# A hybrid decoder layer on one core: three small inputs in one transfer, and another order of the instructions

## The chip, the cores and the metric

The kernel runs on 1 core of one Trainium2 chip. The metric is the device time of one execution in microseconds (us), the median of several runs; lower is better. The engines of the core are TensorE (PE; matrix products and transposes), VectorE (DVE), ScalarE (ACT), GpSimd (POOL) and SyncE (SP), which only issues transfers here.

## The reference

One layer over 1024 tokens of width 1024, in float32:

```python
mod = einsum('bd,de->be', silu(c), w_ada) + b_ada
shift, scale, gate = split(mod, 3)
h = rms_norm(x, norm_w) * (1.0 + scale) + shift
proj = einsum('bsd,de->bse', h, w_in)             # 2888 columns
u_pool, g_pool, q, k, v, g_attn, qi, ki, wi = split(proj, ...)
pool_out = pool_mixer(u_pool, w_pool, pool_scale) * silu(g_pool)
q = rope(rms_norm(q, q_norm_w)); k = rope(rms_norm(k, k_norm_w))
qi = rope(qi); ki = rope(ki)
# dsa_attention, per block of 128 queries (8 heads of 64 over 2 key/value heads):
score = einsum('bqhs,bqh->bqs', relu(qi . ki), wi)  # causal
sel = top_k(score, 256)                             # keys that a query may use
attn_out = softmax(q . k over sel) @ v * silu(g_attn)
y = concatenate([pool_out, attn_out]) @ w_out
x = x + gate * y
```

The pooling mixer takes causal means over windows of 2, 4, 8 and 16 tokens, less the token itself, and one 128 x 128 map for each of 4 groups.

## The kernel before, in words

Tokens are worked on in 8 tiles of 128, or in halves of 512 columns (tiles 4 to 7 first, then 0 to 3). Products that must stay exact are split: a value is cast to its high part (`wh`, `hhi`, `qsh`, `mph`, `xh`) and the rest is the low part (`wl`, `hlo`, `qsl`, `mpl`, `xl`), and each product is three: hi by hi, hi by lo, lo by hi.

Nothing of the order on the engines is written out. Each part of the work is a generator ("strand") that hands its next instruction to a planner, the class `Flow`. The planner keeps a clock for each engine and a cost for each instruction, and issues the one that can start first, corrected by numbers: `EARLY` (by strand, or by strand and its count), `LAST` and `SAFE` (for PE), `FAVOUR` (where an instruction may go to DVE, ACT or POOL, `Either`), `COLD` (until when PE counts as slow), `HOP`, `PHOP`, `STT`, `SWITCH` (small costs), `XB`, `FK`, `MIX`, `AHEAD` (how far loads, products and buffers may run ahead). So a change of one number can move instructions anywhere, and which engine takes one of an `Either`. All instructions are issued from one line of a helper, L238 in the profile of before.

The work goes in this order:

- **Head.** The x tiles 7 to 4 (`xr`) are loaded, squared and summed (`sq`), scaled by their RMS and transposed on PE (`m<-c,xr`). The adaLN sums run on DVE, one pass over each `wada` tile (`wa`), two tiles for each of 8 blocks j; `lead_loads` (L612) issues these pairs, and puts the loads of the x tiles 3 to 0 ahead of pair j = `XB`. `query_loads` brings the weights of the lead line (`ld<-wq`). With shift and scale, h becomes `hhi` and `hlo`, and the lead line multiplies them by the index-query weights: 512 columns for the first half, 256 for part of the second. `c`, `norm_w` and `b_ada` are loaded as `cT`, `nwT` and `badaT`.
- **Keys, values and index queries.** `wkh`, `wkl` by `hhi`, `hlo` give keys, values, index keys (`st`, then `twice` and `kiT`) and index weights. The index queries (`qix`, 4 tiles of 768 columns) are rotated: a shuffle `sw<-qix`, a product with cos, one with sin and the sum, then split into `xh`, `xl`.
- **Gates, queries, mixers.** `ORDER` sets their sequence. Meanwhile, index scores are summed, and the 256 best keys found by bisection: passes that count keys over a limit (`junk` on DVE for tiles 2, 3 and 4: 384, 512 and 640 columns; `ajunk` on ACT for tiles 5, 6 and 7), with small steps (`aq`, `yq`, `xq`) between. For each query group e, the squares are summed on PE: `m<-qsh,c` and `m<-qsl,c`, from a half's `qsh` cast and `qsl` difference. The sums of q2, q1 and q0 follow each other, q0's first. The mixers use `u`, `nx`, `gp` and end in `mph`, `mpl`.
- **Attention** of units 0 to 7: products `m<-kT,qr`, maxima and masking on DVE (`ex`, `mx`), exponentials on ACT (`ex`), transposes (`m<-c,ex`), copies of them (`pw`), products with v, gates (`gt`, `st`, `mah`, `mal`).
- **Output.** `m<-mph,wh` and the like for the pooled half, `m<-mah,wh` for the attended, added into `xo` on DVE.

Of the kernel before, what the change touches and what calls it, by code (L numbers as in the profile page):

```python
# [27 lines left out]
ORDER = "a0 a2 a1 q2 q1 | q0 m1 q3 m2 m3 m0 a3"  # L28
SWAP16 = [(i + 16) % 32 for i in range(32)]
GROUPS = (((5, 6, 7), True), ((2, 3, 4), False))  # L30
# [32 lines left out]
         "lead_out 1": -0.38, "shift 8": 1.56, "out 7": -0.3, "unit 3": -1.17, "turns 3": -3.11,
         "key_value_out 1": -2.25, "exps 4": -0.27, "mix 2": -0.2, "exps 2": 0.46, "out 6": -0.73, "gated 8": -2.42,
         "out 5": -2.76, "token_turns": -1.26, "token_out 9": -0.19, "h_half 14": -0.44, "h_half 10": -0.92,
# [1557 lines left out]
```

## Time and profile before

| what | value |
|---|---|
| time, median of 3 runs | 511.67 us (511.54 to 512.37) |
| profiled execution, its own time | 511.55 us |
| its span in the trace | 509.7 us |
| granted clock of PE, mean | 0.99 |
| busy: PE, DVE, ACT, POOL | 482.0, 417.9, 381.8, 152.0 us |
| moved by transfers | 58.36 MB, mean 114 GB/s |

The span is what the profiler sees of one execution; the time holds 1.85 us more around it. Busy times are averages over very different stretches. The granted clock says at which of two levels PE ran: 1.00 is 2.4 GHz and 0.50 is 1.2 GHz.

### The profile page before, as it was taken

The page shows a single profiled execution, that of the slowest core. Times are in us where ns is not written, and L with a number is a line of the kernel's source. Part 1 is how long each engine was busy: PE and PEld are TensorE (multiplying, and loading weights), DVE is VectorE, ACT ScalarE, POOL GpSimd, SP SyncE. Part 2 cuts the span into 40 slices and gives each one's busy share as a digit, 9 for nine tenths or more (in the row PEclk, how much of TensorE's full clock was granted, in tenths as well). Part 3 has the DMA queues.
Part 4 walks back from the last instruction along what each step waited for, and adds up shares of the span by engine and source line. Part 5 has one row for each costly group of instructions (what it writes and reads, how often), then busy time and mean ns, then how long its engine had stood idle before and what let it go on. Part 6 is the DMA issues. An engine that isn't in the chain of part 4 may idle for free.

```text
span 509.7 us, 8516 instructions
## 1 busy us (share of the span) xinstructions
PE 482.0 (95%) x2912; PEld 361.2 (71%) x2912; DVE 417.9 (82%) x910; ACT 381.8 (75%) x879; POOL 152.0 (30%) x182
## 2 busy tenths in 40 slices
PE   1899999999999989999999998999998999998996
PEld 1678999776768857877887775886675648654485
DVE  5977897799789789989999999978989896666342
ACT  3896541697778999999935999899997666669410
POOL 3597062002001133476131236613521232400000
PEclk9899999999999999999999999999998999999999
DMA  8998503010205112111120013675632134421054
GB/s 300 410 408 311 185 14 119 22 54 31 76 8 186 42 42 84 41 42 42 42 65 27 34 42 92 198 270 163 186 107 64 34 112 124 166 63 43 1 168 163
DMA packets 27884, 58.36 MB, mean 114 GB/s; under 512 B 3776, under 2 KB 7872, under 8 KB 27840
## 3 DMA queue, kind: packets, MB, share of 16 engines
q1 hardware_dynamic: 27840, 57.81, 33.3%
q8 instruction: 23, 0.38, 0.3%
q14 instruction: 21, 0.17, 0.1%
HBM read 47.32 MB, written 10.49 MB: 113 GB/s over the span
## 4 chain that ended last, share of the span: by engine, by line
PE 82%; DVE 8%; DMA 5%; ACT 3%; issue 1%; POOL 0%; SPq 0%; DVEq 0%
PE m L238 82%; DMA wa<-wada 4%; DVE ex L238 3%; ACT ex L238 2%; DVE junk L238 1%; DMA xr<-xR 1%; DVE selw L238 1%; DVE mpl L238 0%; DVE wa L238 0%; DVE mx L238 0%; DVE xq L238 0%; DVE xo L238 0%; DVE gp L238 0%; DVE st L238 0%; POOL qsl L238 0%
## 5 line engine op out<-in xcount | busy, mean ns | idle before, releaser
L238 PE MATMUL m<-hhi,wh 128*128 128x512 f32 (+1 forms) x320 | 120.0, 397 | 1.7 <-ACT xt L238 1.0
L238 PE MATMUL m<-hlo,wh 128*128 128x512 f32 (+1 forms) x320 | 115.2, 383 | 0.0
L238 PE MATMUL m<-hhi,wl 128*128 128x512 f32 (+1 forms) x320 | 115.0, 383 | 0.0
L238 ACT ACTIVATE ajunk<-key,xq 128x768 bf16<-128x768 uint16 (+2 forms) x93 | 96.4, 1036 | 1.5 <-DVE xq L238 0.3
L238 PEld LDWEIGHTS m<-hhi,wh 128*128 128x128 f32 x320 | 58.8, 188 | 18.5 <-issue 4.3
L238 POOL TENSOR_TENSOR wl<-ld,wh 128x512 fp32r<-128x512 f32 x42 | 60.5, 1443 | 38.2 <-ACT wh L238 18.8
L238 DVE TENSOR_SCALAR_CACHE_REDUCE junk<-key,xq 128x384 bf16<-128x384 uint16 (+2 forms) x93 | 69.2, 744 | 2.3 <-DVE xq L238 0.2
L238 PEld LDWEIGHTS m<-hhi,wl 128*128 128x128 f32 x320 | 59.2, 190 | 12.4 <-issue 1.7
L238 PEld LDWEIGHTS m<-hlo,wh 128*128 128x128 f32 x320 | 58.9, 190 | 11.8
L238 ACT ACTIVATE ex<-ex,mx,c 128x384 f32<-128x384 f32 (+7 forms) x64 | 54.9, 860 | 6.4 <-DVE mx L238 4.3
L238 DVE SCALAR_TENSOR_TENSOR score<-kt,c,score 128x1024 f32<-128x1024 f32 (+5 forms) x42 | 40.7, 970 | 7.1 <-ACT kt L238 4.9
L238 ACT ACTIVATE kt<-m 128x512 f32<-128x512 f32 (+1 forms) x80 | 37.7, 525 | 10.9 <-DVE score L238 5.0
L238 PE MATMUL m<-kT,qr 64*128 64x512 f32 (+3 forms) x192 | 40.0, 516 | 1.0 <-DVE mx L238 1.0
L238 DVE SCALAR_TENSOR_TENSOR xo<-m,c,xo 128x512 f32<-128x512 f32 x24 | 18.0, 750 | 25.4 <-PE m L238 18.4
L238 ACT CAST wh<-ld 128x512 fp32r<-128x512 f32 x31 | 19.2, 624 | 23.8 <-DMA ld<-wout 7.5
L238 DVE CUSTOM_DVE_ANT_0 ex<-m,key 128x512 f32<-128x512 f32 (+1 forms) x48 | 30.8, 662 | 5.0 <-PE m L238 4.8
L238 PE MATMUL m<-pw,vrow 128*64 128x512 f32 x144 | 33.3, 604 | 0.0
L238 POOL TENSOR_SCALAR wh<-ld 128x512 fp32r<-128x512 f32 x26 | 17.5, 672 | 51.7 <-PE m L238 33.4
L238 PEld LDWEIGHTS m<-kT,qr 64*128 64x128 f32 x192 | 20.4, 190 | 16.1 <-issue 10.6
L238 ACT COPY pw<-m 128x512 f32<-128x512 f32 x51 | 26.5, 595 | 5.7 <-PE m L238 5.5
L238 PEld LDWEIGHTS m<-c,ex 64*128 64x128 f32 x576 | 21.0, 138 | 10.9 <-DVE mx L238 3.7
L238 PE MATMUL m<-c,ex 64*128 64x64 f32 x576 | 24.0, 226 | 3.8 <-DVE mx L238 1.8
(198 smaller groups left out, 1025.6 us busy)
## 6 DMA issues: line engine op xcount, KB each, us to landing
wa<-wada SPq DMA_DIRECT2D x24, 512.0 KB, 9.3
ld<-wet SPq DMA_DIRECT2D x16, 512.0 KB, 3.4
ld<-wout SPq DMA_DIRECT2D x24, 256.0 KB, 3.2
xr<-xR SPq DMA_DIRECT2D x8, 512.0 KB, 7.3
xo<-xT SPq DMA_DIRECT2D x16, 256.0 KB, 3.8
y_d<-xo SPq DMA_DIRECT2D x16, 256.0 KB, 2.4
xo<-y_d SPq DMA_DIRECT2D x16, 256.0 KB, 3.2
outT<-xo SPq DMA_DIRECT2D x16, 256.0 KB, 2.4
```

The lines of the kernel that those rows point to most:

```text
L238: self.fn(*self.args, **self.kw)
```

## The change

Three small inputs become one array of 128 rows and 40 columns (c in columns 0 to 7, norm_w in 8 to 15, b_ada in 16 to 39), loaded by one transfer in the place of the first. The arithmetic stays, and PE has the same number of matmuls. The rest of the diff changes numbers of the planner. `ATT` (with `turn_of` and `firsts`) writes down the order of the attention units and of the two output halves, which is the one of before.

```diff
-ORDER = "a0 a2 a1 q2 q1 | q0 m1 q3 m2 m3 m0 a3"
+ORDER = "a0 a2 a1 q1 q2 | q0 m1 q3 m2 m3 m0 a3"
+ATT = "0 1 2 3 4 5 6 7"
...
-         "mix": -0.33, "rotated": 0.23, "query_loads": 0.21, "exps": -0.11, "score_sums": -1.07,
+         "mix": -0.33, "rotated": 0.62, "query_loads": 0.2, "exps": -0.11, "score_sums": -1.07,
...
-COLD = 17.877
+COLD = 18.869
-XB = 2
+XB = 3
...
-FK = 0
+FK = 1
-MIX = 5
+MIX = 4
-AHEAD = 4
+AHEAD = 5
-FAVOUR = {"DVE": 0.245, "ACT": -0.111, "POOL": 0.27}
+FAVOUR = {"DVE": 0.267, "ACT": -0.111, "POOL": 0.27}
...
-    c_sb = const([P, 8], F32)
+    c_all = const([P, 40], F32)
+    c_sb, nw_sb, bada_sb = c_all[:, 0:8], c_all[:, 8:16], c_all[:, 16:40]
-    nw_sb = const([P, 8], F32)
-    bada_sb = const([P, 24], F32)
...
-                yield SP.dma_start(c_sb, cT)
-        yield SP.dma_start(nw_sb, nwT)
-        yield SP.dma_start(bada_sb, badaT)
+                yield SP.dma_start(c_all, cT)
```

Of the changed numbers, some 70 stand in `EARLY`, `SAFE` and `LAST`. What they do shows in the order on the engines. Rows of before name line L238, rows of the change L241; the numbers behind names are those of buffers, and differ between the two.

**SP's queue in the head.** From `nwT` (c_77) to the last of the x tiles 3 to 0, before:

```order
L238 DMA c_78<-badaT 128x24
L238 DMA wa_147<-wada 128x1024
L238 DMA wa_149<-wada 128x1024
L238 DMA ld_151<-wq 128x1024
L238 DMA wa_152<-wada 128x1024
L238 DMA wa_159<-wada 128x1024
L238 DMA xr_161<-xR 128x1024
L238 DMA xr_166<-xR 128x1024
L238 DMA xr_173<-xR 128x1024
L238 DMA xr_176<-xR 128x1024
L238 DMA wa_274<-wada 128x1024
```

and in the change, from the first wada pair on:

```order
L241 DMA xr_112<-xR 128x1024
L241 DMA wa_143<-wada 128x1024
L241 DMA wa_145<-wada 128x1024
L241 DMA ld_147<-wq 128x1024
L241 DMA wa_148<-wada 128x1024
L241 DMA wa_153<-wada 128x1024
L241 DMA wa_258<-wada 128x1024
L241 DMA wa_260<-wada 128x1024
L241 DMA ld_262<-wq 128x1024
L241 DMA xr_263<-xR 128x1024
L241 DMA xr_269<-xR 128x1024
```

The two small transfers are gone, and the third wada pair (wa_258, wa_260) and the wq tile ld_262 stand ahead of the x tiles (xr_263 on) now, not behind them. On PE, 32 lead products of 512 columns stand between the first transposes and the second, where 20 did.

**POOL at the index queries**, behind the last work of the lead line, before:

```order
L238 TENSOR_TENSOR wl_619<-ld_474,wh_618 128x512
L238 TENSOR_TENSOR sw_751<-sw_751,sin_538 128x768
L238 TENSOR_TENSOR qix_726<-qix_726,sw_751 128x768
L238 TENSOR_TENSOR wl_856<-ld_712,wh_855 128x512
L238 TENSOR_TENSOR wl_898<-ld_742,wh_897 128x512
L238 TENSOR_TENSOR wl_921<-ld_742,wh_920 128x512
```

and in the change:

```order
L241 TENSOR_TENSOR hlo_650<-xt_440,hhi_649 128x512
L241 TENSOR_TENSOR qix_732<-qix_732,cos_500 128x768
L241 TENSOR_TENSOR sw_741<-sw_741,sin_502 128x768
L241 TENSOR_TENSOR qix_749<-qix_749,cos_500 128x768
L241 TENSOR_TENSOR sw_766<-sw_766,sin_502 128x768
L241 TENSOR_TENSOR qix_732<-qix_732,sw_741 128x768
L241 TENSOR_TENSOR qix_749<-qix_749,sw_766 128x768
L241 TENSOR_TENSOR qix_722<-qix_722,cos_500 128x768
L241 TENSOR_TENSOR sw_746<-sw_746,sin_502 128x768
L241 TENSOR_TENSOR wl_934<-ld_719,wh_933 128x512
```

POOL had two products of the rotations, of one index query (qix_726), and now has eight, of three index queries. DVE keeps the shuffles, the sum for qix_722 and the fourth index query.

**DVE at the norms of q0**, from the cast of its first half to the cast of its second half and what follows, before:

```order
L238 CAST qsh_1964<-st_2025 128x512
L238 TENSOR_TENSOR qsl_1965<-st_2025,qsh_1964 128x512
L238 TENSOR_SCALAR junk_2028,cq_315_2017<-key_83,xq_312_2010 128x512
L238 TENSOR_SCALAR junk_2044,cq_315_2017<-key_84,xq_312_2010 128x640
L238 TENSOR_TENSOR aq_324_2055<-cq_315_2017,kcq_250_1779 128x3
L238 SCALAR_TENSOR_TENSOR xq_325_2056<-aq_324_2055,yq_326_2057 128x3
L238 TENSOR_SCALAR junk_2077,cq_330_2076<-key_82,xq_325_2056 128x384
L238 TENSOR_SCALAR junk_2079,cq_330_2076<-key_83,xq_325_2056 128x512
L238 CAST qsh_1964<-st_2091 128x512
L238 TENSOR_SCALAR junk_2084,cq_330_2076<-key_84,xq_325_2056 128x640
L238 TENSOR_SCALAR yq_341_2102<-xq_325_2056 128x3
```

and in the change:

```order
L241 CAST qsh_1959<-st_2030 128x512
L241 TENSOR_TENSOR qsl_1960<-st_2030,qsh_1959 128x512
L241 TENSOR_TENSOR aq_317_2020<-cq_311_2003,kcq_248_1775 128x3
L241 SCALAR_TENSOR_TENSOR xq_318_2021<-aq_317_2020,yq_319_2022 128x3
L241 TENSOR_SCALAR junk_2050,cq_323_2049<-key_80,xq_318_2021 128x384
L241 TENSOR_SCALAR junk_2060,cq_323_2049<-key_81,xq_318_2021 128x512
L241 TENSOR_SCALAR junk_2063,cq_323_2049<-key_82,xq_318_2021 128x640
L241 TENSOR_TENSOR aq_332_2079<-cq_323_2049,kcq_248_1775 128x3
L241 CAST qsh_1959<-st_2093 128x512
L241 TENSOR_TENSOR qsl_1960<-st_2093,qsh_1959 128x512
L241 SCALAR_TENSOR_TENSOR xq_333_2080<-aq_332_2079,yq_334_2081 128x3
```

Before, the second cast (qsh_1964<-st_2091) stood between two scans (junk) of a pass, and its difference qsl was POOL's. Now the cast (qsh_1959<-st_2093) stands behind a whole pass, and the difference follows it on DVE. Between this cast and the second `mpl` (the one for which PE waits at 318 us), DVE issues one scan of 640 columns, three `yq`, one `nx` of 1016 columns, one `wl` and one `aq` less than before, and three `qsl` and one `wh` more.

Near the end, DVE's `gt` of unit 5, which stood just ahead of the last maxima of unit 6's heads, now stands behind four of them, and two copies of `pw` of the last unit go from DVE to ACT.

## Rows read from the trace of the kernel before

**Rows 1.** The page: busy time of each engine; the chain that ended last.
```profile
PE 482.0 (95%) x2912; PEld 361.2 (71%) x2912; DVE 417.9 (82%) x910; ACT 381.8 (75%) x879; POOL 152.0 (30%) x182
...
PE 82%; DVE 8%; DMA 5%; ACT 3%; issue 1%; POOL 0%; SPq 0%; DVEq 0%
```

**Rows 2.** Windows: stretch, length, busy us of each engine (instructions), granted clock, DMA share, GB/s.
```profile
24.00:60.00 36.00, 34.60 (x246) 29.38 (x245) 27.90 (x52) 26.67 (x44) 22.53 (x20) 1.00 0.84 307
...
30.00:100.00 70.00, 69.68 (x456) 63.71 (x456) 57.37 (x86) 39.06 (x89) 28.15 (x20) 1.00 0.47 166
...
190.00:305.00 115.00, 114.98 (x492) 90.34 (x490) 110.46 (x244) 99.46 (x249) 43.55 (x57) 0.99 0.14 46
305.00:320.00 15.00, 12.67 (x66) 9.15 (x65) 14.61 (x48) 14.87 (x38) 9.32 (x7) 1.00 0.39 110
```

**Rows 3.** Timeline of PE, head: start us, duration, engine, instruction, idle before.
```profile
25.27 0.72 PE L238 MATMUL m<-c,xr 64*128 64x64 f32 x16 [0.49 <-POOL xr L238]
...
59.11 0.32 PE L238 MATMUL m<-wkh,hhi 128*128 128x328 f32 x1
```

**Rows 4.** Timeline of PE at the first query norms.
```profile
188.24 0.39 PE L238 MATMUL m<-qsh,c 128*8 128x512 f32 x1 [0.75 <-DVE qsh L238]
189.59 0.45 PE L238 MATMUL m<-qsl,c 128*8 128x512 f32 x1 [0.95 <-POOL qsl L238]
189.84 0.63 PE L238 MATMUL m<-qsh,c 128*8 128x512 f32 x1
...
193.24 0.39 PE L238 MATMUL m<-hhi,wh 128*128 128x512 f32 x1
```

**Rows 5.** Waits of PE, 305 to 320 us: total us, times, longest.
```profile
PE m L238 <- DVE mpl L238: 1.4, 1, 1.4
PE m L238 <- DVE mx L238: 1.0, 2, 0.5
```

**Rows 6.** Waits of PE, 436 to 490 us.
```profile
PE m L238 <- ACT ex L238: 1.3, 2, 0.8
```

**Rows 7.** Timeline of SP's queue (SPq), its DMA issues in the head.
```profile
3.12 0.44 SPq L238 DMA_DIRECT2D c<-nwT  x1
3.60 0.43 SPq L238 DMA_DIRECT2D c<-badaT  x1
...
16.07 4.17 SPq L238 DMA_DIRECT2D wa<-wada  x4
```

**Rows 8.** Timeline of DVE, 12.67 us.
```profile
12.67 1.21 DVE L238 SCALAR_TENSOR_TENSOR wa<-wa,m 128x1024 f32<-128x1024 f32 x1
```

**Rows 9.** Timeline of POOL, DVE, ACT and PE around the index queries.
```profile
63.60 2.62 POOL L238 TENSOR_TENSOR sw<-sw,sin 128x768 f32<-128x768 f32 x1 [13.57 <-DVE sw L238]
...
88.53 1.63 DVE L238 TENSOR_TENSOR st<-st,rows 128x128 f32<-128x128 f32 x5 [2.75 <-ACT st L238]
...
90.97 1.06 ACT L238 COPY twice<-st 128x1024 f32<-128x1024 f32 x1 [2.39 <-DVE st L238]
...
93.25 0.92 PE L238 MATMUL m<-c,twice 128*128 128x128 f32 x7
```

**Rows 10.** Timeline of DVE and POOL at the query norms.
```profile
182.71 0.69 DVE L238 TENSOR_TENSOR qsl<-st,qsh 128x512 fp32r<-128x512 f32 x1
...
187.76 0.42 DVE L238 CAST qsh<-st 128x512 fp32r<-128x512 f32 x1
...
188.26 1.27 POOL L238 TENSOR_TENSOR qsl<-st,qsh 128x512 fp32r<-128x512 f32 x1 [1.88 <-DVE qsh L238]
```

**Rows 11.** Groups of DVE by form, 186 to 316 us: busy us, mean ns, idle before.
```profile
L238 DVE TENSOR_SCALAR_CACHE_REDUCE junk<-key,xq 128x640 bf16<-128x640 uint16 x24 | 21.1, 878 | 0.5
...
L238 DVE TENSOR_SCALAR yq<-xq 128x3 f32<-128x3 f32 x3 | 1.9, 631 | 0.0
...
L238 DVE TENSOR_TENSOR nx<-nx 128x1016 f32<-128x1016 f32 x1 | 1.2, 1212 | 0.0
```

**Rows 12.** Timeline of DVE, 438.60 us.
```profile
438.60 0.68 DVE L238 TENSOR_TENSOR gt<-gt,m 128x512 f32<-128x512 f32 x1
```

More of the change, by code (lines that the diff above doesn't have):

```diff
@@ L44 @@
+         "key_value_out": -1.34, "index_queries": -0.86, "norm": -0.31, "gate_loads": -1.2, "token_scales": -3.22,
+         "gate_mods": -0.39, "unit": -1.06, "index_scores": -1.07, "lead_loads": 1.31, "out": -1.44,
+         "lead_out": -0.62, "weight_loads": 0.29, "key_value_weights": -1.29, "main_line": 0.11, "output_line": 1.37,
          "turns": -1.46, "finish": -1.64, "index_keys": -1.47, "h_block": 0.28, "attention_keys": -0.36,
-         "turned": -1.0, "h_blocks": -0.59, "gated": -2.15, "modulations": 0.89, "low": 0.65, "gear": 0.42,
@@ L63 @@
[L63 to L65 removed]
[6 rows of a table added]
+         "key_value_out 6": -2.24, "norm 1": -1.96, "gear 4": -1.05, "products": -1.29, "shift 4": -0.32,
+         "norm 5": -1.64, "low 1": -2.52, "turns 6": -2.43, "gated 6": -2.43, "turns 8": -1.76, "h_block 3": -0.55,
@@ L75 @@
+         "token_out 13": -0.78, "token_out 5": -0.25, "h_half 7": -0.24, "token_tile 7": -0.74, "token_tile": -0.49,
+         "unit 5": 0.1, "unit 1": -0.94, "h_half 5": -0.42}
 SELECT = -0.425
-LAST = {"main": 0.12, "fill": -0.081, "scores": 0.035, "attend": -0.104, "evac": -0.027, "qi": 0.257,
-        "side": -0.376}
-SAFE = {"side": 1.0, "unit": 0, "query_norms": 0.69, "h_block": 0.59, "rotated": 0.48, "query_loads": 0,
-        "norm": 0.29, "weight_loads": 0.85, "key_value_out": 0.39, "turned": 0.26, "finish": 0, "index_keys": 0.85,
+LAST = {"main": 0.12, "fill": -0.081, "scores": 0.035, "attend": -0.104, "evac": -0.106, "qi": 0.257,
+        "side": -0.237}
@@ L81 @@
+SAFE = {"side": 1.0, "unit": 0, "query_norms": 0, "h_block": 0.59, "rotated": 0.48, "query_loads": 0,
+        "norm": 0.29, "weight_loads": 1.12, "key_value_out": 0.39, "turned": 0.26, "finish": 0, "index_keys": 1.01,
         "main_line": 0, "output_line": 0, "gate_mods": 1.06, "selection": 0, "low": 0.27, "maxima": 0,
-        "attention": 0.44, "lead_out": 0, "score_relus": 0, "lead_loads": 0.28, "score_sums": 0.18, "mix": 0.96,
-        "main": 0, "modulations": 0.09, "out": 0.39, "turns": 0.34, "exps": 0, "lead_line": 1.22, "shift": 0,
@@ L91 @@
+        "weight_splits": 0, "token_turns": 0, "gear": 0, "key_value_weights": 0}
+COLD = 18.869
+XB = 3
 WKM = 8
 HOP = 0.103
-PHOP = -0.1
-STT = 0.071
+PHOP = -0.148
+STT = 0.073
 HOPS = {"PE": 0.19, "DVE": 0.13, ("ACT", "DVE"): 0.14, ("ACT", "ACT"): 0.035}
-SWITCH = {"all": 0.1, "rows": 0.28, "columns": 0.29}
+SWITCH = {"all": 0.1, "rows": 0.28, "columns": 0.27}
 AGE = 0.37
@@ L1278, in hybrid_layer @@
     mixa, gate, done, normed, ended = {}, {}, [], [], []
+    turn_of = [int(i) for i in ATT.split()]
+    firsts = [c for c in (0, 1) if turn_of[-1] // 4 != c]
     main_over = []
@@ L1285, in gate_loads @@
         yield lambda: len(gates_out) == 8
-        for i in range(NT):
-            yield lambda: len(ended) >= i - 1
+        for n, i in enumerate(turn_of):
+            yield lambda: len(ended) >= n - 1
             t = yield big(w=512, s="gt", keep=keep)
@@ L1293, in attention @@
         yield lambda: kT and len(queries_out) == 4 and normed_q
-        for i in range(NT):
-            yield lambda: i in masks and len(ended) >= i - FLY
+        for n, i in enumerate(turn_of):
+            yield lambda: i in masks and len(ended) >= n - FLY
             flow.spawn(unit(i), "attend")
@@ L1365, in turns @@
         def turns():
-            yield lambda: len(done) >= i
+            yield lambda: len(done) >= turn_of.index(i)
             flow.spawn(products(), "attend")
@@ L1460, in project_attended @@
         cs = slice(c * 512, (c + 1) * 512)
-        yield lambda: len(ended) >= 4 * c + 4 and len(pooled_out) == 16
+        yield lambda: all(i in ended for i in range(4 * c, 4 * c + 4)) and len(pooled_out) == 16
         hi, lo = ([mixa[c][g][t][:, e * 512:(e + 1) * 512] for g in range(2) for e in range(2)] for t in range(2))
@@ L1492, in output_line @@
         yield from project_pooled()
-        yield from project_attended(0)
-        yield from project_attended(1)
+        yield from project_attended(firsts[0])
+        yield from project_attended(1 - firsts[0])
     flow.now(constants())
```

33 lines of the change are left out of this document (15 added, 18 removed), and 20 rows, old and new, of the table EARLY.

## The prediction

> **What bounds the kernel now.** I first read the page's busy times and its chain: TensorE (PE) is busy 482.0 of 509.7 us and holds 82% of the chain that ended last; VectorE (DVE) holds 8% and transfers 5% [rows 1]. So the time is PE's work, which the change leaves alone (its count of matmuls stays), plus the places where PE waits or runs at half clock. Then I cut the span into stretches to find those places. From 30 to 100 us PE is busy 69.68 of 70.00 us, from 190 to 305 it is busy 114.98 of 115.00; there, DVE is nearly as full, 110.46 us [rows 2]. What is left over lies in four places, and in each I went to the timeline and the chain of waits:
>
> 1. The head. The second half of the tokens (tiles 3 to 0) is turned on PE from 25.27 us, and the first key/value product (wkh) starts at 59.11 [rows 3]. Between 24 and 60 us PE idles only 36.00 - 34.60 = 1.40 us [rows 2].
> 2. The first query norms. PE waits 0.75 us for DVE's cast qsh and 0.95 us for qsl, which POOL computes; then, from 189.84 to 193.24, eight norm products take 0.425 us each at half clock [rows 4].
> 3. The first attention units and the pooled output, 305 to 320 us. PE waits 1.4 us for mpl and 1.0 us for two maxima, all of them DVE's [rows 5].
> 4. The end of the attention, where PE waits twice for exponentials, 1.3 us together [rows 6].
>
> The profiled execution took 511.55 us, 0.12 below the median of 511.67, so the sum is made on 511.55. A change of under 0.2%, or 1.02 us, can't be told from none.
>
> **The change part by part.**
>
> *The merged transfer.* Two issues on SP go, 0.44 and 0.43 us, 0.87 together [rows 7]. That all of it arrives at the end I don't expect: DVE takes the first wada tile at 12.67 without a wait ahead of it, straight behind its own scaling of x [rows 8], and the tiles follow at the pace of their bytes. Between 0 and 0.87 us, I take 0.4, the middle, for the arrival of later tiles.
>
> *The moved x tiles.* The four loads of x tiles 3 to 0 go behind the third wada pair and one wq tile: on SP's queue three loads of 512 KB each pass them. SP issues four such loads in 4.17 us once the queue is full [rows 7], so one takes (4.17 - 0.43) / 3 = 1.25 us and three 3.74. The second transposes then start 3.74 us later, less the 0.4, at about 28.6. PE isn't idle for all of that, because twelve more of the lead products stand ahead of the transposes in its order now (32 instead of 20). They are 512 columns wide like the norm products, which take 0.425 us at half clock [rows 4], so 0.2125 at full: 2.55 us. From the transposes on the work is as before, less those twelve: 59.11 moves by 3.74 - 0.4 - 2.55 = **+0.8 us**. Bounds: -0.6, if in the new order PE loses none of its 1.40 us of idle time in that stretch; +2.5, if the clock falls once more while PE has work (rival 2). From 30 us on PE has no spare time [rows 2], so this passes on to the end.
>
> *The index-query rotations.* Three sine products, three cosine products and two sums go to POOL or stay there; POOL had two such before, of 2.62 us the first, after 13.57 us with nothing to do [rows 9]. PE is busy with other products to 93 us, so this costs nothing as long as POOL's chain ends in time. What that needs is rival 3.
>
> *The norms of q0.* POOL needed 1.27 us for the second qsl, after DVE's cast of 187.76; DVE needs 0.69 us for the same shape [rows 10]. Now DVE does cast and qsl one after the other, so that the last of them ends near 187.76 + 0.42 + 0.69 = 188.9 instead of 189.5, and PE goes on 0.7 us earlier. Of PE's two waits the second shrinks from 0.95 to about 0.3, and its idle time here from 1.70 to 1.05. In the stretch from 305 to 320 us it idles 1.4 in one piece and 1.0 in two [rows 5], and the granted clock stays at 1.00 [rows 2]. So I expect no fall here, which saves half of 193.24 - 189.84, or 1.7 us: together -2.4. If the clock falls all the same, -0.7.
>
> *What DVE loses after it.* A gain of PE at place 2 holds only if DVE comes earlier at place 3 too, because all PE's waits there are for DVE. DVE hardly idles between [rows 2], so its own sum decides. From the cast of q0's second half to mpl, counted in the order of both kernels, it issues one scan of 640 columns (junk), three yq, one nx of 1016 columns and one wl less: 0.88 + 3 x 0.63 + 1.21 + 0.69 = 4.67 us, the wl at the price of the qsl of the same shape; and three qsl and one wh cast more: 3 x 0.69 + 0.42 = 2.49 us, the wh at the price of the cast qsh [rows 10, 11]. Net -2.2. PE's -2.4 and DVE's -2.2 are nearly the same size, so the waits of place 3 stay as they are, and what reaches the end is the smaller: **-2.2 us**. It is also about this if the clock does fall at place 2, since the waits of place 3 (2.4 us) then shrink by what DVE gains and PE doesn't. Bounds: -2.4, and -0.7 if DVE's gain is eaten up, by waits for ScalarE at the norms of q3 or by POOL's port.
>
> *The tail.* DVE's gt of 0.68 us stood ahead of the maxima of unit 6 at 438.60 [rows 12], and now stands behind four of them; two copies of pw at the end go to ScalarE. Bounds: 0, if ScalarE's exponentials start when PE lets them, and -1.3, both waits of [rows 6]. I take **-0.4**, below the middle, since PE sets the start of most of what ScalarE does there.
>
> Sum: 511.55 + 0.8 - 2.2 - 0.4 = 509.75, so **509.8 us**.
>
> By the Trainium skill ("DMA: Bandwidth & Descriptors", Rules for kernel authors) many small transfers should become one large one, and those under 64 KB are mostly overhead: by it the whole 0.87 would come through, and the sum would be 509.3; the trace shows only that much of issue time on SP, not that it is waited for.
>
> **The rivals.**
>
> *1. Place 2 gives little.* The clock still falls there, and DVE's removed work is filled by waits for ScalarE. Then 511.55 + 0.8 - 0.7 - 0.4 = 511.25, within 0.2%. For it: 0.75 us of the waits at place 2 come from DVE's cast, which now stands behind one more scan. Against it: DVE's own sum.
>
> *2. A second fall in the head.* With x later, PE idles before the second transposes, and if the clock falls when PE has work again, half a stretch like the 3.4 us at place 2 [rows 4] is lost: +1.7, so 511.45, within 0.2%. It needs work without a break from the fall on; before the transposes, PE would wait for x anyway and the loss be hidden.
>
> *3. POOL's rotations come late: slower.* Eight products of 768 columns now stand on POOL before DVE can finish the third index query (qix_722 in the order). At 1.5 times the 1.27 us of 512 columns [rows 10] they take 8 x 1.9 = 15.2 us and end at 63.6 + 15.2 = 78.8. DVE then has nine instructions ahead of its st, of 0.69 us (512 columns) to 1.5 times that (768), some 8.5 us: 87.3, ahead of 88.53, when it started st after waiting 2.75 us for ScalarE. At the 2.62 us that the row of POOL shows, they end at 84.6 and st starts at 93.1, 4.6 late. ScalarE's copy twice, made from st, ended at 92.03, and PE took it at 93.25 [rows 9]: a cushion of 1.2. So PE loses 3.4 us there and all behind it is later: 509.75 + 3.4 = 513.15, slower by 0.3%. It decides from 8.5 + 63.6 + 8 t = 88.53 + 1.2 on, a product of t = 2.2 us. For it: the one row of POOL at this width. Against it: that row lies beside DVE's own products, of which few are left while DVE waits for POOL. The Trainium skill ("GPSIMD Engine Reference", Engine selection) advises against two-input elementwise work on POOL, as about twice as slow as on DVE; the trace agrees at 512 columns, 1.27 against 0.69 us [rows 10]. Twice 1.5 times 0.69 would be 2.1, and the chain just in time.
>
> *4. The merge does all it can.* The whole 0.87 us reaches the second transposes, the rest as in the sum: 509.75 - 0.47 = 509.3.
>
> **How the numbers follow.** The sum as it stands 0.42, rival 4 0.15: faster 0.57. Rivals 1 and 2, 0.13 and 0.09: same 0.22. Rival 3 and the upper bounds of the other terms together 0.21: slower. The lower end is the sum with each term near its better bound, 511.55 - 0.6 - 2.4 - 1.3 = 507.25, so 507.3; the upper end is rival 3, 513.2. The likeliest case alone has 508.7 to 510.6.
>
> **What the profile after would show.** The head: second transposes near 28.6 and the first wkh product near 59.9; if it is under 59.1 or over 61, the term is wrong. POOL: the eight rotations done by 80 us, and no wait of PE between 87 and 97. Place 2: no wait for POOL, and full clock from 187 to 194. Place 3: waits of PE for mpl and the maxima of the same size, 2.4 us together, but 1.4 us earlier. Tail: gt behind the maxima, and a shorter wait for exponentials near 470. The prediction falls if DVE is late at q0's cast, which would show as a longer first wait at place 2 and longer ones at place 3.

## The result: slower by 0.8%

The changed kernel takes 516.18 us (median of 6 runs, 515.25 to 517.10); the kernel before, in the same measurement, 511.61 (6 runs, 509.97 to 512.37). The ratio is 1.0083, with a 95% interval of 1.0064 to 1.0102, where 509.8 us had been forecast. The profiled execution of the changed kernel took 515.25 us, with a span of 513.5; that of before has 509.7. So 3.8 us are to be found between the two traces.

The page of the changed kernel, busy times and the chain that ended last:

```profile
PE 481.1 (94%) x2912; PEld 360.3 (70%) x2912; DVE 415.7 (81%) x901; ACT 383.4 (75%) x884; POOL 160.8 (31%) x185
...
PE 66%; DVE 21%; ACT 5%; DMA 3%; issue 2%; POOL 1%; SPq 0%; DVEq 0%; POOLq 0%
```

PE does no more than before [rows 1], yet its share of the chain went from 82 to 66%, and DVE's from 8 to 21%: PE now waits for DVE in more places. The windows of the changed kernel (columns as in rows 2) show where:

```profile
24.00:60.00 36.00, 34.29 (x232) 28.64 (x231) 32.50 (x53) 26.26 (x44) 18.53 (x17) 0.95 0.80 295
30.00:100.00 70.00, 68.29 (x458) 61.96 (x456) 50.79 (x78) 40.16 (x90) 37.44 (x25) 1.00 0.46 165
190.00:305.00 115.00, 111.12 (x480) 87.33 (x480) 111.57 (x239) 97.93 (x245) 44.09 (x55) 1.00 0.14 44
305.00:320.00 15.00, 14.18 (x72) 10.30 (x71) 14.44 (x49) 14.87 (x39) 5.97 (x9) 1.00 0.25 80
```

From 190 to 305 us PE was busy in all but 0.02 us before [rows 2]; now it lacks 3.88 of 115. Of this, 1.01 us are the waits of q0's norms, which before ended ahead of 190 us; the rest is new. The timeline of PE names the waits (start, duration, instruction, idle time ahead of it and what ended that):

```profile
23.20 1.41 PE L241 MATMUL m<-hhi,wh 128*128 128x512 f32 x4 [2.56 <-ACT hhi L241]
...
29.58 0.59 PE L241 MATMUL m<-c,xr 64*128 64x64 f32 x12
...
61.68 0.31 PE L241 MATMUL m<-wkh,hhi 128*128 128x328 f32 x1
...
190.71 0.40 PE L241 MATMUL m<-qsh,c 128*8 128x512 f32 x1 [0.68 <-DVE qsh L241]
191.44 0.40 PE L241 MATMUL m<-qsl,c 128*8 128x512 f32 x1 [0.33 <-DVE qsl L241]
...
228.49 1.13 PE L241 MATMUL m<-u,c 128*128 128x512 f32 x2 [0.76 <-DVE u L241]
231.32 0.39 PE L241 MATMUL m<-qsl,c 128*8 128x512 f32 x1 [1.00 <-DVE qsl L241]
...
268.60 1.98 PE L241 MATMUL m<-u,c 128*128 128x512 f32 x4 [1.10 <-DVE u L241]
...
316.81 2.00 PE L241 MATMUL m<-kT,qr 64*128 64x128 f32 x12 [0.53 <-DVE mx L241]
319.07 1.46 PE L241 MATMUL m<-kT,qr 64*128 64x256 f32 x6 [0.26 <-DVE mx L241]
322.71 0.50 PE L241 MATMUL m<-mpl,wh 128*128 128x512 f32 x1 [1.52 <-DVE mpl L241]
```

Beside [rows 3]: the second transposes come 4.31 us later (25.27 to 29.58) and the first wkh product 2.57 later. Beside [rows 4]: q0's norms wait 0.68 + 0.33 us, where it was 0.75 + 0.95, and no half clock follows. But three waits behind them, at 228, 231 and 268 us, stand in no row of the trace before. Beside [rows 5]: the waits for mpl and the maxima are as long as they were, 2.3 us, and 4.0 us later.

All kernels of this study were profiled, and their PE timelines compare in a simple way. Where a stretch and what lies ahead of it are in the old order, the time between two landmarks repeats to 0.1 us, but for falls of the granted clock, which come at another place in each execution. In the changed order the last stretch doesn't repeat (62.11 to 63.65 us in nine kernels), and s2_only and s3_only show that a stretch can also depend on what lies ahead of it. The landmarks are the starts of the first product of a kind; "fall" marks, behind wkh, a stretch of half clock within:

| kernel | to wkh | q0's first qsh to first qn | qn to first mpl | mpl to first mah | mah to unit 7's last kT |
|---|---|---|---|---|---|
| before | 59.11 | 49.97 (fall) | 81.84 | 81.84 (fall) | 61.65 |
| merge_only | 60.50 | 49.64 | 81.87 | 81.75 (fall) | 61.67 |
| x_late | 63.55 | 49.60 | 81.83 | 80.20 | 61.64 |
| qsl_dve | 59.55 | 49.84 | 81.84 | 80.19 | 61.64 |
| changed | 61.68 | 49.97 | 83.34 | 80.28 | 63.03 |
| new_rest | 60.25 | 49.95 | 83.30 | 80.22 | 63.55 |
| wl_later | 61.96 | 49.97 | 81.98 (fall) | 80.24 | 63.65 |
| s2_only | 59.71 | 49.95 | 82.66 | 81.78 (fall) | 61.66 |
| s3_only | 60.19 | 49.97 (fall) | 81.96 | 80.25 | 61.65 |
| tail_only | 60.90 | 49.61 | 81.82 (fall) | 82.06 (fall) | 62.56 |

So the changed order loses in four stretches: the head, q0's norms to qn (+0.33 beside merge_only), qn to mpl (+1.47) and the end of the attention (+1.36). From wkh to q0's norms (127.7 us) and from unit 7's last kT to PE's last product (43.3) all kernels agree. The head's start scatters by 2 us from run to run: eight kernels with the old head have wkh at 59.11 to 61.28, mean 60.19, and eight with the new one, hhi_first among them, at 61.68 to 62.52, mean 62.14, so +1.95. The four make 5.1 us, beside 4.6 between the medians.

### The profile page after: what moved, and what is told of

It is laid out like the page before. It is cut to its first block, busy times and chain, and to the rows that moved or that the text cites. A ratio compares the mean times of both kernels' runs of the same rounds, so it can differ in the third digit from the quotient of the medians.

```text
span 513.5 us, 8513 instructions
## 1 busy us (share of the span) xinstructions
PE 481.1 (94%) x2912; PEld 360.3 (70%) x2912; DVE 415.7 (81%) x901; ACT 383.4 (75%) x884; POOL 160.8 (31%) x185
## 4 chain that ended last, share of the span: by engine, by line
PE 66%; DVE 21%; ACT 5%; DMA 3%; issue 2%; POOL 1%; SPq 0%; DVEq 0%; POOLq 0%
PE m L241 66%; DVE junk L241 4%; DVE ex L241 3%; DMA ld<-wq 2%; ACT ex L241 2%; DVE wa L241 2%; DVE sw L241 1%; DVE selw L241 1%; DMA xr<-xR 1%; DVE nx L241 1%; DVE hlo L241 1%; DVE u L241 1%; DVE qr L241 1%; DVE aq L241 1%; DVE mpl L241 1%
## 5 line engine op out<-in xcount | busy, mean ns | idle before, releaser
L241 PE MATMUL m<-hhi,wh 128*128 128x512 f32 (+1 forms) x320 | 119.4, 396 | 2.8 <-ACT hhi L241 2.6
L241 PE MATMUL m<-hlo,wh 128*128 128x512 f32 (+1 forms) x320 | 115.3, 384 | 0.9 <-DVE hlo L241 0.7
L241 PE MATMUL m<-hhi,wl 128*128 128x512 f32 (+1 forms) x320 | 114.5, 383 | 0.0
L241 ACT ACTIVATE ajunk<-key,xq 128x768 bf16<-128x768 uint16 (+2 forms) x93 | 96.4, 1036 | 1.1
L241 POOL TENSOR_TENSOR wl<-ld,wh 128x512 fp32r<-128x512 f32 x42 | 57.0, 1359 | 47.3 <-ACT wh L241 27.2
L241 PEld LDWEIGHTS m<-hhi,wh 128*128 128x128 f32 x320 | 58.3, 188 | 19.1 <-issue 3.5
L241 DVE TENSOR_SCALAR_CACHE_REDUCE junk<-key,xq 128x384 bf16<-128x384 uint16 (+2 forms) x93 | 69.2, 744 | 2.1
L241 PEld LDWEIGHTS m<-hlo,wh 128*128 128x128 f32 x320 | 59.0, 190 | 13.7 <-DVE hlo L241 1.2
L241 PEld LDWEIGHTS m<-hhi,wl 128*128 128x128 f32 x320 | 58.9, 190 | 12.3 <-issue 1.4
L241 ACT ACTIVATE ex<-ex,mx,c 128x384 f32<-128x384 f32 (+7 forms) x64 | 54.9, 861 | 7.3 <-DVE mx L241 7.2
L241 ACT ACTIVATE kt<-m 128x512 f32<-128x512 f32 (+1 forms) x80 | 37.9, 525 | 11.2 <-DVE score L241 5.3
L241 DVE SCALAR_TENSOR_TENSOR score<-kt,c,score 128x1024 f32<-128x1024 f32 (+5 forms) x42 | 39.9, 950 | 6.9 <-ACT kt L241 4.9
L241 DVE SCALAR_TENSOR_TENSOR xo<-m,c,xo 128x512 f32<-128x512 f32 x25 | 18.8, 750 | 27.9 <-PE m L241 21.9
L241 PE MATMUL m<-kT,qr 64*128 64x512 f32 (+3 forms) x192 | 39.1, 504 | 0.8 <-DVE mx L241 0.8
L241 DVE CUSTOM_DVE_ANT_0 ex<-m,key 128x512 f32<-128x512 f32 (+1 forms) x48 | 30.9, 662 | 6.0 <-PE m L241 5.8
L241 ACT CAST wh<-ld 128x512 fp32r<-128x512 f32 x33 | 20.3, 619 | 19.7 <-PE m L241 12.2
L241 ACT COPY pw<-m 128x512 f32<-128x512 f32 x54 | 28.2, 604 | 8.0 <-PE m L241 5.3
L241 PE MATMUL m<-pw,vrow 128*64 128x512 f32 x144 | 32.9, 599 | 0.0
L241 PEld LDWEIGHTS m<-kT,qr 64*128 64x128 f32 x192 | 19.3, 186 | 16.3 <-issue 10.0
L241 PEld LDWEIGHTS m<-c,ex 64*128 64x128 f32 x576 | 21.5, 139 | 11.4 <-DVE mx L241 4.0
L241 PE MATMUL m<-c,ex 64*128 64x64 f32 x576 | 24.5, 227 | 4.4 <-DVE mx L241 1.8
L241 PE MATMUL m<-kiT,xh 64*128 64x512 f32 (+3 forms) x160 | 27.1, 378 | 0.3 <-ACT kt L241 0.3
```

The source lines that it names most:

```text
L241: self.fn(*self.args, **self.kw)
```

## The experiments

The kernels of the experiments have the planner's steps written out as a list, so that one step can be moved or a stretch taken from the other list; with an unmoved list the instructions on each engine are those of the kernel before or of the changed kernel. BEFORE and CHANGED are these lists of 2135 and 2134 steps. All were timed in 5 rounds beside the kernel before.

### The parts of the head

**merge_only.** The kernel before, with the merged transfer alone:

```diff
-yield SP.dma_start(c_sb, cT)
+yield SP.dma_start(c_all, cT)        # 40 columns
...
-yield SP.dma_start(nw_sb, nwT)
-yield SP.dma_start(bada_sb, badaT)
```

> The order of every engine as before; only the three small inputs come in one transfer of 40 columns. Theory (the merge is hidden): 511.2 to 511.9, the first wada pass on DVE not more than 0.4 us earlier than 12.67, the first wkh product within 0.4 us of 59.1. Rival (small transfers cost their whole overhead): 510.7, all of the head 0.9 us earlier.

Measured: 511.72 us, ratio 0.9991 (0.9971 to 1.0011). Its second transposes start at 25.99 us, not earlier than before; its wkh, expected within 0.4 us of 59.1, comes at 60.50, inside the scatter of the head. The 0.87 us of issue time is worth nothing that can be measured; the forecast had taken 0.4 for it.

**new_head.** The changed order up to the first wkh product, from there that of before.

```diff
-PLAN = CHANGED
+PLAN = CHANGED[:281] + (steps of BEFORE not done yet)
```

> Up to the first wkh product the order of the change (merged transfer, x tiles 3 to 0 behind the third wada pair), from there on the order of before. Theory (the head by itself costs what the first wkh product is late, 2.55 us, and nothing behind it takes it back): first wkh product near 61.7, time 514.1. Rival (the loss of the head is swallowed by later waits, so that the 4.6 us of the change come from behind the head): 512.5 or less with the first wkh product still near 61.7.

Measured: 513.80 us, ratio 1.0026 (1.0007 to 1.0045). The wait for hhi is there, 2.55 us, and behind wkh every stretch is as before. The head costs 1.3 us.

**hhi_first.** The changed kernel; ACT makes shift and high half of block 2 ahead of the two casts and the first square.

```diff
+ACT  ACTIVATE c (shift of block 2)
+ACT  ACTIVATE hhi<-xt
 ACT  CAST wh<-ld
-ACT  ACTIVATE c (shift of block 2)
 ACT  CAST wh<-ld
 ACT  ACTIVATE sq<-xr
-ACT  ACTIVATE hhi<-xt
```

> The changed kernel; on ACT alone, the shift and the cast hhi of block 2 stand ahead of two casts of wq weights and of the squares of an x tile, where they stood behind them. Theory (PE's wait of 2.56 us at 23.2 is ACT's queue and not the late x tiles): that wait falls under 0.5 us, the first wkh product comes 1.5 to 2.5 us earlier than 61.7, time 513.7 to 514.7. Rival (the second transposes wait for x, whatever ACT does first): second transposes at 29.0 or later, first wkh product over 61.0, time 515.5 or more.

Measured: 517.82 us, ratio 1.0100 (1.0066 to 1.0133), wkh at 62.52. The theory that ACT's queue made the loss falls. The wait only changed its name:

```profile
25.94 2.08 PE L362 MATMUL m<-hlo,wh 128*128 128x512 f32 x4 [2.50 <-DVE hlo L362]
```

The second transposes came no earlier (30.45).

**x_late and x_early.** SP alone, in one direction and the other: the kernel before with the four x loads behind the third wada pair and a wq tile, and the changed kernel with them ahead of it.

```diff
-XB = 2
+XB = 3        # x_late, other engines as before; x_early is the reverse in the changed kernel
```

> The kernel before with SP alone changed: the four x tiles are loaded behind the third wada pair and one wq tile, all other engines in the old order. If the arrival of x sets the second transposes, they go from 25.3 to 28.5 to 30 us, and without the twelve lead products ahead of them PE loses all of it: the first wkh product at 62 to 63, and 514 to 515.5 us. If x has slack, 511.5 to 512.5.

> The changed kernel with SP alone put back: the four x tiles are loaded ahead of the third wada pair again, all other engines in the changed order. If the head is late because x comes late, the second transposes go back from 29.6 to 26 to 28 us and the time falls by 1 to 2 us, to 514.2 to 515.2. If the changed order of the other engines needs the third wada pair where it was, PE waits for a shift or a high half instead, the first wkh product stays at 61.5 or later, and the time is 516 or more.

Measured: x_late 514.17 us, ratio 1.0058 (1.0037 to 1.0079); x_early 521.62, ratio 1.0195 (1.0170 to 1.0221). In x_late, ACT's first square of these tiles waits for the transfer:

```profile
21.80 1.06 ACT L359 ACTIVATE sq<-xr 128x1024 f32<-128x1024 f32 x1 [4.12 <-DMA xr<-xR]
```

So x has no slack, and its second transposes start at 29.71, as in the changed kernel. There, without the reordering around it, the move costs 3.0 us; the changed order takes back about half. That x sets the second transposes in the changed order too is seen in two kernels with its head, apart and wl_later (below). In the changed kernel PE runs at half clock from 24.0 us on and comes to these transposes without a wait; in those two it stays at full clock there and waits 1.16 and 1.21 us for x instead. In apart:

```profile
29.78 0.71 PE L362 MATMUL m<-c,xr 64*128 64x64 f32 x16 [1.16 <-POOL xr L362]
```

The start, 29.78 and 29.89 us, is as late as in the changed kernel. In x_early the products that now stand ahead of the transposes lack the third wada pair:

```profile
28.49 2.07 PE L362 MATMUL m<-hhi,wh 128*128 128x512 f32 x4 [7.61 <-ACT hhi L362]
```

Each order goes with its own place of the loads, and the new pair is the worse one.

### The rest of the program

**new_rest.** The order of before up to wkh, then the changed one.

```diff
-PLAN = BEFORE
+PLAN = BEFORE[:278] + (steps of CHANGED not done yet)
```

> The kernel before up to the first key/value product, with its three small transfers and its early x tiles, and from there on the order of the changed kernel. If the changed order loses at two places, in the head (some 1.5 us) and behind the query norms (some 2.5 us: DVE's longer instructions, the waits at 439 to 445), this takes 513.5 to 515 us, with the first wkh product near 60 and PE's waits at mpl as in the changed kernel. If the whole loss is made in the head, it is within 0.7 us of the kernel before, 511.3 to 512.7.

Measured: 513.96 us, ratio 1.0058 (1.0033 to 1.0083): the larger part of the loss is behind the head. 1.0058 and new_head's 1.0026 make 1.0084, beside 1.0083 for the whole.

**s2_only, s3_only, tail_only.** The kernel before with the changed order in one stretch.

```diff
-PLAN = BEFORE
+PLAN = BEFORE[:403] + CHANGED[403:980] + BEFORE[980:]      # s2_only, ORDER and MIX of the change
+PLAN = BEFORE[:980] + CHANGED[980:1339] + BEFORE[1339:]    # s3_only, MIX of the change
+PLAN = BEFORE[:1827] + CHANGED[1827:]                      # tail_only
```

> The kernel before with the changed order only from some 90 to 236 us: the rotations on POOL, q0's and q3's norms and qsl. If the 0.7 us that q0's norms gain is taken back by the wait for u at 228 and for q3's qsl at 231, the pooled queries (qn) come as late as before and the time is within 0.6 us of it, 511.0 to 512.2. By the forecast's step the gain would stay: 509.4 to 510.4.

> The kernel before with the changed order only from 236 us to the first attention units. If DVE's key of 640 columns meets a wl on POOL there and makes the second u late, PE waits 1.0 us near 267, qn to mpl takes 83.3 us in place of 81.85, and the time is 512.6 to 513.6. If DVE has the slack that it has in the kernel before, because the part ahead is the old one, the collision does no harm: 511.0 to 512.2.

> The kernel before with the changed order only from 435 us on (from the last exponentials of unit 6 to the end). If this stretch carries a loss of its own, PE waits near 439 us for DVE's xo and POOL's st, the last unit's products come 1 to 1.5 us later, and the time is 512.3 to 513.3 us beside 511.6. If those waits were only a consequence of what lies ahead of them in the changed kernel, or the forecast's 0.4 us of gain is real, it is 511.0 to 511.9.

Measured: s2_only 512.23 us, ratio 1.0016 (1.0001 to 1.0030); s3_only 511.59, ratio 1.0009 (0.9992 to 1.0026); tail_only 513.29, ratio 1.0033 (1.0014 to 1.0053). In s2_only the norms are quicker and q3's qsl later, and qn comes as late as in the changed kernel, so the gain doesn't stay. Its order differs from the old one only from 115 us on, so the rotations on POOL, which the expectation names, aren't in it. Behind qn, where its order is the old one again, it loses another 0.8 us (82.66): there DVE's key starts 0.63 us behind a wl on POOL and takes 1.47 us. s3_only has no wait near 267 and loses nothing that can be measured: that stretch costs only where the part ahead of it has brought DVE and POOL into step (below). The three ratios together make 1.0058, as in new_rest. tail_only costs 1.7 us, more than its profile shows (0.9).

The tail was expected to show a wait for xo. It doesn't; of the changed kernel's waits at this place only that for POOL's st is there. Among the nine kernels with this order the wait for xo goes from none (apart, tail_only) to 1.39 us (wl_later), and the stretch from 62.11 to 63.65 with it. PE's timeline in the changed kernel:

```profile
439.12 0.71 PE L241 MATMUL m<-c,ex 64*128 64x64 f32 x15 [0.77 <-DVE xo L241]
441.63 0.66 PE L241 MATMUL m<-c,st 128*128 128x128 f32 x4 [0.21 <-POOL st L241]
```

in tail_only:

```profile
440.26 0.66 PE L359 MATMUL m<-c,st 128*128 128x128 f32 x4 [0.31 <-POOL st L359]
```

The first mah group and the norm's transposes are the same in both orders, but 48 transposes of ex now stand ahead of them where 32 did, and the norm's wide copy is POOL's instead of ACT's.

**turns_back.** The changed kernel with the last 16 of those 48 put back behind the output product and the norm.

```diff
-PE   TRANSPOSE m<-c,ex x16
 PE   MATMUL m<-mah,wh; mah,wl; mal,wh (twice)
 PE   TRANSPOSE m<-c,st x4
+PE   TRANSPOSE m<-c,ex x16
```

> The changed kernel with one group of transposes of unit 6 (x48 of ex, with two output products and one norm around it) put back behind the output product and the norm, where the kernel before has it. PE waited 0.77 us there for a bank that DVE frees with an xo (439.12) and three times 0.2 behind it. If this order makes the loss of 1.5 us between 406 and 445, the first of these waits goes and the time falls by 0.5 to 1.5 us, to 514.7 to 515.7. If it is noise of one execution or made up behind it, the time stays within 0.5 us of 516.2.

Measured: 518.75 us, ratio 1.0148 (1.0120 to 1.0177), worse. The wait for xo is gone, but without the transposes as cover PE meets POOL's copy sooner:

```profile
441.02 0.66 PE L362 MATMUL m<-c,st 128*128 128x128 f32 x4 [1.18 <-POOL st L362]
```

Then it waits 0.72 us for ACT's pw, and in this profile the granted clock is at 0.50 from 443.4 to 446.8 us. So of the tail it is shown that the stretch loses by itself, but no single edit was found that gives it back. ACT's copy put back as well wasn't tried.

### DVE beside POOL

**qsl_dve and merge_qsl.** The kernel before with q0's second qsl on DVE; merge_qsl has the merged transfer too.

```diff
 DVE  CAST qsh<-st
-POOL TENSOR_TENSOR qsl<-st,qsh
+DVE  TENSOR_TENSOR qsl<-st,qsh
```

> The order of before; one instruction moves: the qsl of q0's second half goes from POOL to DVE, straight behind its cast. Theory (DVE is the bound from here to the mpl at 316 us): PE resumes 0.7 us earlier at the norms, but its waits from there to 319 us grow by at least as much, and by 0.7 us of DVE's added work; time 511.6 to 512.4. Rival (what PE gains at the norms stays gained, as predicted): 0.7 us less, and 2.4 if the half-clock stretch goes too, 509.2 to 510.9.

> The kernel before with the two parts of the change that cost nothing: one transfer for c, norm_w and b_ada, and q0's second qsl on DVE; all orders are those of before. Alone they gave ratios of 0.9991 and 0.9981. If they add, 510.2 us beside 511.6 (ratio 0.997); if the clock and the later waits swallow them, 511 to 511.8.

Measured: qsl_dve 510.88 us, ratio 0.9981 (0.9962 to 1.0000); merge_qsl 511.72, ratio 1.0004 (0.9982 to 1.0026). qsl_dve by itself lies in the rival's range, at the edge of what can be told from none, but its profile has no gain: 49.84 us to qn, beside 49.64 in merge_only. Together no gain is left that can be told from none. PE's waits show why, first in merge_only, with qsl on POOL:

```profile
189.62 0.39 PE L359 MATMUL m<-qsh,c 128*8 128x512 f32 x1 [0.75 <-DVE qsh L359]
190.96 0.39 PE L359 MATMUL m<-qsl,c 128*8 128x512 f32 x1 [0.95 <-POOL qsl L359]
226.84 1.12 PE L359 MATMUL m<-u,c 128*128 128x512 f32 x2 [0.95 <-DVE u L359]
```

and in qsl_dve:

```profile
188.70 0.40 PE L359 MATMUL m<-qsh,c 128*8 128x512 f32 x1 [0.75 <-DVE qsh L359]
189.43 0.40 PE L359 MATMUL m<-qsl,c 128*8 128x512 f32 x1 [0.33 <-DVE qsl L359]
226.14 1.12 PE L359 MATMUL m<-u,c 128*128 128x512 f32 x2 [1.80 <-ACT aq L359]
```

The step from qsh to qsl shrinks by 0.61 us (1.34 to 0.73), and 37 us later PE waits 0.85 us longer ahead of its products of u. The profile puts this wait down to ACT's aq; DVE's u ends at the same time, at 226.1 us.

**qsl_pool.** The changed kernel with q3's two qsl back on POOL.

```diff
-DVE  TENSOR_TENSOR qsl<-st,qsh     (q3, both halves)
+POOL TENSOR_TENSOR qsl<-st,qsh
```

> The changed kernel with the two qsl of q3 back on POOL, where the kernel before has them; q0's stays on DVE. DVE issues 0.69 and 1.66 us less. If the qsl on DVE are what DVE lacks at mpl, PE's waits at 231 and 268 us shrink and that for mpl falls below 0.8: 514 to 515.5 us. If POOL's qsl come late behind its wl, the wait at 231 grows to 1.5 or more and the time stays at 516 or above.

Measured: 516.37 us, ratio 1.0094 (1.0067 to 1.0122). The wait at 231 falls to 0.66 us and qn comes 0.47 us earlier, but the one at 268 stays (0.97) and that for mpl is 1.52 again, to the digit, against the expectation. The waits of 0.53, 0.26 and 1.52 us there are the same in qsl_pool, apart, u_apart and the changed kernel. That doesn't mean that DVE's two qsl cost nothing: PE waits for DVE's mx just ahead of mpl, so the last wait is only what DVE does between mx and mpl. The stretches tell more. From q0's cast to mpl DVE takes 128.88 us, beside 129.47 in the changed kernel, and PE takes 132.72 from q0's first qsh to mpl, beside 133.31: the 0.6 us that DVE saves do arrive at mpl. The time of the whole doesn't show them.

**apart and u_apart.** The changed kernel; in apart q3's second qsl and the second u each stand behind the next scan, in u_apart only the u.

```diff
+DVE  TENSOR_SCALAR junk 128x640
 DVE  SCALAR_TENSOR_TENSOR u<-nx,u
-DVE  TENSOR_SCALAR junk 128x640
```

> The changed kernel with two instructions of DVE moved, each behind a scan that it does not depend on: q3's second qsl behind the next scan of 384 columns, and the second u behind the next scan of 640. Both started within 0.5 us of a wl on POOL and took 1.66 and 2.33 us. If it is the start beside POOL's two-operand work that makes them long, they fall to 0.7 to 0.9 and 1.2 us, DVE is some 1.5 to 2 us earlier at mpl, PE's wait there of 1.5 us nearly goes, and the time is 514.3 to 515.3. If they are long for another reason, or if DVE does not set the end there, the time stays at 515.7 to 516.7.

> The changed kernel with only the second u moved behind the next scan of 640 columns; q3's qsl stays where it was. u, which took 2.33 us beside a wl on POOL, should take 1.2, and PE's wait of 1.10 us for it at 268.6 should go, without the later qsl and the wait of 2.00 us that moving qsl had made. If DVE's collisions with POOL cost time, 514.7 to 515.7 us; if PE's lost time there is made up at mpl anyway, the same 1.1 us shows as a longer wait at mpl and the time stays at 516.2 within 0.5.

Measured: apart 517.20 us, ratio 1.0117 (1.0085 to 1.0150); u_apart 517.09, ratio 1.0098 (1.0065 to 1.0130). In apart, qsl takes 0.69 us again, but aq of 3 columns now stands beside the wl and takes 1.23, and PE waits longer for the later qsl:

```profile
232.99 0.40 PE L362 MATMUL m<-qsl,c 128*8 128x512 f32 x1 [2.00 <-DVE qsl L362]
```

In its profile the half clock follows at once. Key takes 0.49 us there, and the wait at 268 is gone. In u_apart key is long (1.63), u ends no earlier, and the wait stays 1.10: the u was not the culprit, the key ahead of it was.

**wl_later.** So the next kernel moved POOL's instruction, not DVE's.

```diff
-POOL TENSOR_TENSOR wl<-ld,wh 128x512     (at 262.85)
 POOL TENSOR_SCALAR yq<-xq 128x3
+POOL TENSOR_TENSOR wl<-ld,wh 128x512
```

> The changed kernel with one wl on POOL (the one at 262.85) issued behind POOL's next yq, so that it starts some 1.9 us later; nothing else is moved. If the 1.58 us of DVE's key and the 2.33 of its u come from starting beside POOL's wl, key takes 0.5 us, u starts 1.1 us earlier and takes 1.2, PE's wait of 1.10 us at 268.6 goes and qn to mpl takes 82.2 us: 514.7 to 515.5. If they are long anyway, 516.2 within 0.5.

The rows of POOL and DVE in the changed kernel, where wl starts 0.06 us ahead of key and 0.22 ahead of u:

```profile
262.85 1.29 POOL L241 TENSOR_TENSOR wl<-ld,wh 128x512 fp32r<-128x512 f32 x1 [4.15 <-ACT wh L241]
...
266.00 1.47 POOL L241 TENSOR_TENSOR wl<-ld,wh 128x512 fp32r<-128x512 f32 x1 [1.19 <-ACT wh L241]
...
262.91 1.58 DVE L241 TENSOR_TENSOR key<-selw 128x640 uint16<-128x640 uint16 x1
...
266.22 2.33 DVE L241 SCALAR_TENSOR_TENSOR u<-nx,u 128x1024 f32<-128x1024 f32 x1
```

and in wl_later, with PE behind them:

```profile
263.96 1.29 POOL L362 TENSOR_TENSOR wl<-ld,wh 128x512 fp32r<-128x512 f32 x1
...
263.18 0.49 DVE L362 TENSOR_TENSOR key<-selw 128x640 uint16<-128x640 uint16 x1
...
265.42 1.21 DVE L362 SCALAR_TENSOR_TENSOR u<-nx,u 128x1024 f32<-128x1024 f32 x1
...
267.61 1.88 PE L362 MATMUL m<-u,c 128*128 128x512 f32 x4
```

Nothing is shorter on POOL; it only starts later, and DVE's key and u lose 1.09 and 1.12 us. PE's wait of 1.10 us is gone, and qn to mpl takes 81.98 us where 82.2 was expected. From q0's cast to mpl DVE takes 128.65 us, 0.82 less than in the changed kernel, and at mpl PE waits 0.46 us instead of 1.52. Ahead of that it waits 1.60 us for ACT's st and runs at half clock from 316.9 to 320.9 us. Measured: 514.09 us, ratio 1.0069 (1.0040 to 1.0099). The interval overlaps that of the changed kernel; the stretch is what tells.

In s3_only the same pairs start in the other order, wl 0.20 us behind key and 0.08 behind u:

```profile
261.33 1.44 POOL L359 TENSOR_TENSOR wl<-ld,wh 128x512 fp32r<-128x512 f32 x1 [4.41 <-ACT wh L359]
264.48 2.27 POOL L359 TENSOR_TENSOR wl<-ld,wh 128x512 fp32r<-128x512 f32 x1 [1.52 <-ACT wh L359]
...
261.13 0.49 DVE L359 TENSOR_TENSOR key<-selw 128x640 uint16<-128x640 uint16 x1
264.40 1.22 DVE L359 SCALAR_TENSOR_TENSOR u<-nx,u 128x1024 f32<-128x1024 f32 x1
```

Here DVE loses nothing, and POOL's second wl takes 2.27 us instead of 1.29. In the kernel before, key starts 0.13 us ahead of wl (260.13 and 260.26) and takes 0.49 as well. So tenths of a microsecond between the two starts decide which engine waits.

## Why the prediction was wrong

The bound was read rightly: PE's work stayed, and the loss lies in the waits. Most of the new waits stand outside the four places, though, at 228, 231, 268 and 439 us. Term by term:

- **The merged transfer** (0.4 of 0.87 us taken): nothing that can be told from none, 0.9991. That was inside its bounds.
- **The moved x tiles** (+0.8): mis-sized, +1.95 by the means of the profiles, 1.3 us by new_head's time. The transposes went 4.31 us later where 3.34 were forecast: SP issued the four x loads from 9.57 us on in 1.75 us before, and now from 11.05 in 4.17, so the last ended at 11.32 and 15.22, the first square on ACT moved by the same (17.36 to 21.30), and the merge gave nothing back. And the twelve products credited with 2.55 us didn't fill the gap, since PE waits 2.56 us for the high half of its second block ahead of them. The credit supposed that their operands are there; x_early and hhi_first show that the wada passes and halves behind them have no slack either.
- **The rotations on POOL:** right, and rival 3 didn't come. The eight end at 81.7 us, 2.0 each, below the 2.2 from which it decided; `twice` moved by 2.56 us, like wkh.
- **The norms of q0:** right on the spot, 1.01 us of idle time where 1.05 was forecast, and full clock behind. But the 1.7 us counted for the clock weren't there to win. In merge_only the same waits aren't followed by half clock, and from q0's first qsh to qn it takes 49.64 us, where before took 49.97 with it: the half clock costs 0.33 us there, because PE has to wait for u at 226 us in any case (0.95).
- **What DVE loses after it** (-2.2): this is the step that failed, in its sum more than in its mechanism. That DVE decides when PE gets past mpl holds: what DVE saves between q0's cast and mpl in qsl_pool and wl_later, PE gains there (0.6 and 0.6 us in the first; 0.82 and 1.36 in the second, where mpl itself is 0.54 us shorter). The waits of place 3 stayed as they were, too, as forecast. But -2.2 was DVE's sum by durations of the trace before, and it came out as a loss. From q0's cast to mpl DVE took 128.26 us before (187.76 to 316.02) and takes 129.47 (190.23 to 319.70), 1.2 more; in that, its busy time (the third of the engines) rose by 2.4:

```profile
187.76:316.02 128.26, 125.84 (x549) 98.19 (x549) 123.30 (x291) 112.62 (x282) 50.40 (x64) 0.99 0.14 46
...
190.23:319.70 129.47, 124.97 (x547) 97.34 (x547) 125.70 (x287) 112.28 (x281) 49.76 (x63) 1.00 0.15 48
```

  The durations were at fault: a qsl of 1.66 us where 0.69 was counted, a key of 1.58 for 0.49 and a u of 2.33 for 1.2, each started just behind a wl on POOL. They make 3.2 of the 4.6 us between -2.2 and +2.4; wl_later shows the cause for key and u, apart for qsl, and the rest wasn't taken apart. That all of PE's waits behind place 2 stand at place 3 was wrong as well: there are waits between, at u, qsl and u again, where PE stands just behind DVE, and in them the gain of place 2 is gone (49.97 us from q0's first qsh to qn, before and after). "POOL's port" stood in the prediction as one bound (-0.7), as a gain eaten up and not as a loss.
- **The tail** (-0.4): wrong in sign; 1.7 us slower by itself. I counted DVE's gt and not PE's sixteen transposes moved ahead, nor the copy that goes to POOL.

The Trainium skill ("SBUF — State Buffer", Who interferes with whom) states that a DVE instruction with two SBUF inputs and a GpSimd one that reads SBUF share a port pair by a lock, and that issue order decides which waits in full. The trace agrees: key beside a wl that started 0.06 us earlier took 1.58 us, and 0.49 us where wl started later; in s3_only, where u started first, it was wl that took 2.27. It is the rule that spoke against this change, and the prediction weighed it only as a bound.

Of the rivals, the first came nearest: place 2 gives little, but for the waits behind it and not by the clock. The second's fall came, at 24.0 us, but no cost of it shows: apart and wl_later have none in the head, and their wkh (62.39 and 61.96) is no earlier than 61.68. The range ended at 513.2, since its only slow mechanism was POOL being late; that DVE could be late was looked for at q0's cast, and it came 37 us behind it.

What stays open: which edit gives the tail's 1.7 us back, and how much of the head's loss another order of DVE could save, and what else made DVE's stretch to mpl longer. No version is faster than the kernel before by more than the noise; qsl_dve (0.9962 to 1.0000) comes nearest.

## What to carry to other kernels

- A gain at one wait is worth what the next wait lets through: here 0.61 us won at q0's norms met a wait 0.85 us longer at u. Follow the engine onwards to the next place where it stands close behind the same producer.
- When work moves between DVE and POOL, don't price it by the durations of the old trace alone. Look at which two-input instructions will start beside each other, and give the sum a loss bound of one POOL instruction for each pair.
- Don't count a fall of the clock in one profile as a cost of that place. See whether a wait behind it hides it.
